# Strassen products in alternating half order, an earlier split, two more tiles and a two-queue start, in a one-layer hybrid trunk

## The chip, the cores and the metric

The kernel runs on one core of one Trainium2 chip. The metric is the device time of one launch in microseconds. Five engines work side by side, each through its own queue in order: TensorE (PE, with its weight loads shown apart as PEld), VectorE (DVE), ScalarE (ACT), GpSimd (POOL) and SyncE (SP). SP only issues DMAs here; ACT and POOL issue some of their own.

## The reference, cut to what matters

One layer over 512 tokens of width 2048, in fp32: a token mixer (one input projection, split between a gated DeltaNet group of 8 heads and a gated short convolution, then an output projection), cross-attention of 4 heads into 256 memory tokens, and a feed-forward part with a width-3 causal convolution.

```python
h = rmsnorm(x, mix_norm);  proj = h @ w_mix_in
y_gdn = gdn_group(proj, gdn_conv, a_log, dt_bias, out_gain)   # conv4 + silu, l2norm, gated delta rule in chunks
y_sc  = b_gate * causal_dwconv(c_gate * hh, sc_conv)
x = x + concat([y_gdn, y_sc]) @ w_mix_out
h = rmsnorm(x, xattn_norm);  mem_n = rmsnorm(mem, mem_norm)
x = x + softmax((h @ w_q) @ (mem_n @ w_k).T * d**-0.5) @ (mem_n @ w_v) @ w_o   # by heads
h = rmsnorm(x, ffn_norm)
u = causal_dwconv(h @ w_up, conv_w);  gate, up = split(u)
x = x + (silu(gate) * up) @ w_down
return rmsnorm(x, final_norm)
```

## The kernel before

Every large matrix product is made in three (or, for products of halves of the tokens, two and a half) passes: a 128x1024 piece of weights `wst` is loaded by DMA, rounded by ACT to a high part `whi` (L523, L146), and DVE subtracts to get the low part `wlo` (L524, L147). The pools hold three `whi`, three `wlo` and five `wst` buffers, so the splitting can run at most three pieces ahead of TensorE. The activations are kept as a 128x512 operand that holds a high part (columns 0 to 255) beside a low part (256 to 511).

`mm2s` (L168) multiplies one piece of eight 128x128 blocks: first eight matmuls of `whi` against all 512 columns (the "wide" ones, L172), then eight of `wlo` against the 256 high columns (the "narrow" ones, L175).

The program goes through these stages, in order of time:

- **Start** (0 to about 101 us): dummy matmuls `warm` on ones, while the first loads arrive; then the values of the memory, `values` (L357). Its first two tiles alternate wide and narrow matmuls (`mm2`, L165 and L166) on parts split by `early_parts`, in the hand-written order of a `manual_schedule`.
- **Fold of values and output weights** (about 101 to 194 us, L681 to L684).
- **Mixer input projection** (about 194 to 740 us): 28 "quads". A quad takes two column tiles of the weights, 2x2 blocks, and makes the four block results by Strassen's seven products (`quad_left`, `quad_right`, each product through `product` and `mm2s`). The products of a quad use, in turn, the blocks a11, a12, s2, s1, s3, a12 changed, a22; s1, s2 and s3 are sums of blocks, made by DVE (L601, L625) and by accumulating DMAs of POOL (L536, L542). The hooks `between[0]` to `between[3]` run the rest of the quad before (convolutions, gating) at four places of a quad.
- **Keys** (about 740 to 842 us, `psk`), and the **fold of keys and queries** (about 842 to 980 us, `pswk`, L1089, L1091, L1097: all narrow). Each of the 32 pieces of `w_xq` takes half of the sixteen key tiles `kts`: q = 0 uses the first eight, q = 1 the last eight. **Mixer output** follows (`psx1`, about 980 to 1187 us). Woven into these three are the chains of the delta rule, `prepare_chunk`, `invert`, `solve`, `recur`, `scaled`, for two halves `hb` of the heads and four chunks `j`. A chain is a generator: `yield cost, wait` gives the time that its step is thought to take on TensorE, and how long it then stays aside. `tick` and `place` run it between the matmuls once the wait is over. So the waits in these yields set where a step stands in the program.
- **Attention** (about 1188 to 1374 us), then **up projection** of the feed-forward part (about 1374 to 2238 us): 44 quads of the same kind, where `run_held` makes the convolutions and the sums of the quad before, and the down projection (to the end, `psd`, all wide).

Outside the hand-written parts a scheduler with a cost table of its own sets the order on each engine, and it may also move single matmuls of one product ahead of another.

Three names return below. `solve` (L924) loads decay rows into `gb`; for chunk j it takes one of two fixed tiles, `xacc` or `macc`, by j % 2. POOL multiplies by `gb` at the end of `solve` (L970, L971), and only then can the load for chunk j + 2 begin. `tp` is the pool of 64 tiles of 128x512 from which `T` takes. `vn` (L991) is the product in `recur` on which the next matmuls, `pso` (L1000), wait.

## Time and profile before

| | |
|---|---|
| median of 3 runs | 2669.97 us (2668.78 to 2670.71) |
| profiled execution | 2670.58 us, span from first to last instruction 2668.4 us |
| mean granted TensorE clock | 0.997 |
| PE busy | 2649.2 us, 99% |
| PEld busy | 2289.6 us, 86% |
| DVE busy | 2238.2 us, 84% |
| ACT busy | 1570.2 us, 59% |
| DMA | 543.91 MB, mean 204 GB/s |

The busy time of a pipelined PE counts overlapping durations, so it says only that PE hardly ever stands still; how fast matmuls follow each other is read from their starts. In a row of the timeline the first number is the start in us, the second the length of the merged group, then engine, line, operation, output and inputs, shape and count; in brackets stands how long the engine had been idle before, and what ended that.

### The profile page before, as it was taken

The page shows a single profiled execution, that of the slowest core. Times are in us where ns is not written, and L with a number is a line of the kernel's source. Part 1 is how long each engine was busy: PE and PEld are TensorE (multiplying, and loading weights), DVE is VectorE, ACT ScalarE, POOL GpSimd, SP SyncE. Part 2 cuts the span into 40 slices and gives each one's busy share as a digit, 9 for nine tenths or more (in the row PEclk, how much of TensorE's full clock was granted, in tenths as well). Part 3 has the DMA queues.
Part 4 walks back from the last instruction along what each step waited for, and adds up shares of the span by engine and source line. Part 5 has one row for each costly group of instructions (what it writes and reads, how often), then busy time and mean ns, then how long its engine had stood idle before and what let it go on. Part 6 is the DMA issues. An engine that isn't in the chain of part 4 may idle for free.

```text
span 2668.4 us, 40148 instructions
## 1 busy us (share of the span) xinstructions
PE 2649.2 (99%) x14757; PEld 2289.6 (86%) x14757; DVE 2238.2 (84%) x3339; ACT 1570.2 (59%) x2284; POOL 238.6 (9%) x281
## 2 busy tenths in 40 slices
PE   9999999999999999999999999999999999999998
PEld 8888888888888998888888888888888888888886
DVE  7878888999988774466779999999999999877888
ACT  7675555666664674445666665565656555554445
POOL 0000000000110222000000000000000000000202
PEclk9999999999999999999999999999999999999999
DMA  8786667777677985665656767777677676764987
GB/s 302 230 272 188 178 159 187 185 195 189 188 228 229 294 252 168 225 201 191 177 164 168 206 178 185 188 178 202 168 197 184 174 200 202 259 192 143 268 272 185
DMA packets 258549, 543.91 MB, mean 204 GB/s; under 512 B 28064, under 2 KB 119344, under 8 KB 258352
## 3 DMA queue, kind: packets, MB, share of 16 engines
q1 hardware_dynamic: 183488, 396.08, 45.3%
q0 software_dynamic: 30176, 93.36, 20.1%
q10 hardware_dynamic: 44688, 51.92, 5.5%
q8 instruction: 115, 1.88, 0.3%
q14 instruction: 82, 0.67, 0.1%
HBM read 472.83 MB, written 67.39 MB: 202 GB/s over the span
## 4 chain that ended last, share of the span: by engine, by line
PE 96%; DVE 2%; DMA 1%; issue 0%; ACT 0%; SPq 0%; DVEq 0%; ACTq 0%
PE px L172 19%; PE px L175 10%; PE pz L172 10%; PE psd L1513 5%; PE psd L1514 5%; PE psd L1517 5%; PE pz L175 5%; PE py L172 5%; PE psx L157 3%; PE psx L158 3%; PE psx L159 3%; PE py L175 2%; PE psk L1069 2%; PE psk L172 2%; PE psk L1072 1%; PE psmo L681 1%
## 5 line engine op out<-in xcount | busy, mean ns | idle before, releaser
L172 PE MATMUL px<-xo,whi 128*128 128x512 f32 x2288 | 574.1, 393 | 1.7 <-ACT whi L523 1.7
L523 ACT CAST whi<-wst 128x1024 fp32r<-128x1024 f32 x290 | 304.2, 1051 | 323.0 <-PE pz L172 186.2
L172 PEld LDWEIGHTS px<-xo,whi 128*128 128x128 f32 x2288 | 411.6, 189 | 76.8 <-ACT whi L523 2.3
L524 DVE TENSOR_TENSOR wlo<-wst,whi 128x1024 fp32r<-128x1024 f32 x290 | 352.7, 1217 | 24.8 <-ACT whi L523 24.8
L175 PEld LDWEIGHTS px<-xo,wlo 128*128 128x128 f32 x2288 | 312.1, 190 | 22.5 <-DVE wlo L524 0.3
L147 DVE TENSOR_TENSOR wlo<-wst,whi 128x1024 fp32r<-128x1024 f32 x204 | 250.0, 1232 | 90.1 <-ACT whi L146 85.6
L175 PE MATMUL px<-xo,wlo 128*128 128x256 f32 x2288 | 319.2, 282 | 0.0
L523 ACT CAST whi<-s 128x1024 fp32r<-128x1024 f32 x214 | 223.3, 1045 | 157.9 <-DVE wlo L524 82.1
L146 ACT CAST whi<-wst 128x1024 fp32r<-128x1024 f32 x204 | 212.6, 1050 | 145.2 <-PE psx L158 35.5
L172 PE MATMUL pz<-xo,whi 128*128 128x512 f32 x1152 | 289.3, 393 | 0.0
L524 DVE TENSOR_TENSOR wlo<-s,whi 128x1024 fp32r<-128x1024 f32 x214 | 260.4, 1218 | 2.6 <-ACT whi L523 2.4
L1514 PE MATMUL psd<-whi,hdl 128*128 128x512 f32 x616 | 239.8, 389 | 0.0
L1513 PE MATMUL psd<-whi,hdh 128*128 128x512 f32 x616 | 239.8, 389 | 0.0
L172 PEld LDWEIGHTS pz<-xo,whi 128*128 128x128 f32 x1152 | 207.1, 189 | 36.9 <-ACT whi L523 0.2
L1517 PE MATMUL psd<-wlo,hdh 128*128 128x512 f32 x616 | 169.3, 390 | 0.3 <-DVE wlo L1308 0.2
L175 PEld LDWEIGHTS pz<-xo,wlo 128*128 128x128 f32 x1152 | 157.1, 190 | 11.4 <-DVE wlo L524 0.2
L1305 ACT CAST whi<-wst 128x1024 fp32r<-128x1024 f32 x96 | 101.2, 1054 | 108.0 <-issue 46.9
L175 PE MATMUL pz<-xo,wlo 128*128 128x256 f32 x1152 | 160.7, 282 | 0.0
L172 PE MATMUL py<-xo,whi 128*128 128x512 f32 x560 | 140.2, 392 | 0.0
L1517 PEld LDWEIGHTS psd<-wlo,hdh 128*128 128x128 f32 x616 | 115.6, 188 | 25.1 <-DVE wlo L1308 1.1
L1514 PEld LDWEIGHTS psd<-whi,hdl 128*128 128x128 f32 x616 | 115.7, 188 | 24.1 <-DVE hdl L153 0.2
L1513 PEld LDWEIGHTS psd<-whi,hdh 128*128 128x128 f32 x616 | 115.6, 188 | 23.9
(374 smaller groups left out, 4948.4 us busy)
## 6 DMA issues: line engine op xcount, KB each, us to landing
wst<-in_w_up SPq DMA_DIRECT2D x132, 512.0 KB, 4.3
wst<-in_w_dn SPq DMA_DIRECT2D x118, 512.0 KB, 4.5
s<-in_w_up POOLq DMA_DIRECT2D x87, 512.0 KB, 6.2
wst<-in_w_mix SPq DMA_DIRECT2D x84, 512.0 KB, 5.4
s<-in_w_mix POOLq DMA_DIRECT2D x55, 512.0 KB, 6.0
s<-in_w_up SPq DMA_DIRECT2D x43, 512.0 KB, 4.6
hid<-hf_d SPq DMA_DIRECT2D x77, 256.0 KB, 5.2
wst<-in_w_xo SPq DMA_DIRECT2D x32, 512.0 KB, 4.6
```

The lines of the kernel that those rows point to most:

```text
L146: nc.scalar.copy(hi, st)
L147: nc.vector.tensor_tensor(lo, st, f(hi), op=ALU.subtract)
L157: nc.tensor.matmul(ps, wh, xh, start=first, stop=False)
L158: nc.tensor.matmul(ps, wh, xl, start=False, stop=False)
L172: nc.tensor.matmul(ps, hi[:, k * P : (k + 1) * P], x, start=first and k == 0, stop=False, skip_group_check=True)
L175: nc.tensor.matmul(ps[:, n:], lo[:, k * P : (k + 1) * P], x[:, :n], start=False, stop=end, skip_group_check=True)
L523: nc.scalar.copy(hi, t)
L524: tt(lo, t, f(hi), op=ALU.subtract)
L1305: nc.scalar.copy(hi[:, i * n : (i + 1) * n], t)
L1513: nc.tensor.matmul(bs[b], xs[0][:, c], w[0][:, n], start=first, stop=False)
L1514: nc.tensor.matmul(bs[b], xs[1][:, c], w[0][:, n], start=False, stop=False)
L1517: nc.tensor.matmul(bs[b], xs[0][:, c], w[1][:, n], start=False, stop=last)
```

## The change

1. `mm2s` takes a flag `swap`, and `product` flips it at every call. One product does its eight wide matmuls and then its eight narrow ones, the next its eight narrow ones and then its eight wide ones, so that like follows like across the border of two products. The flag is reset to False ahead of the 28 and of the 44 quads. The values at the start keep the old order.
2. In a quad after the first two, s2 is split (`wsplit`) ahead of `between[1]`, where the held convolutions stand.
3. `tp` has 66 tiles, and `solve` takes its decay rows for chunks 2 and 3 from it.
4. The first four pieces of `w_xq` go (0, 0), (1, 0), (0, 1), (1, 1), so that two pieces use the first eight key tiles before any uses the last eight.
5. The steps of `prepare_chunk` for the second half of the heads stay aside 14 after their loads instead of 9, and `invert` of that half starts at 130 instead of 145 in the chains' clock.
6. At the start ACT issues the loads of the first columns and of the first two memory tiles, ahead of its table load and its copy; SP begins with the weights. There are 10 dummy matmuls instead of 12.

```diff
-WARM = 12
+WARM = 10
-    tp = ctx.enter_context(tc.tile_pool(name="tp", bufs=64))
+    tp = ctx.enter_context(tc.tile_pool(name="tp", bufs=66))
-    nc.sync.dma_start(cols[:, :C_FFNN], g["cols"][:, :C_FFNN])
+    nc.scalar.dma_start(cols[:, :C_FFNN], g["cols"][:, :C_FFNN])
-    nc.scalar.copy(cst[:, 2:3], cst[:, 0:1])
-    def mm2s(ps, hi, lo, xs, first, last):
+    def mm2s(ps, hi, lo, xs, first, last, swap=False):
         n = xs[0].shape[1] // 2
-        for k, x in enumerate(xs):
-            nc.tensor.matmul(ps, hi[:, k * P : (k + 1) * P], x, start=first and k == 0, stop=False, skip_group_check=True)
-        for k, x in enumerate(xs):
-            end = last and k == len(xs) - 1
-            nc.tensor.matmul(ps[:, n:], lo[:, k * P : (k + 1) * P], x[:, :n], start=False, stop=end, skip_group_check=True)
+        for low in (swap, not swap):
+            dst, w = (ps[:, n:], lo) if low else (ps, hi)
+            for k, x in enumerate(xs):
+                opens, closes = first and low == swap and k == 0, last and low != swap and k == len(xs) - 1
+                nc.tensor.matmul(dst, w[:, k * P : (k + 1) * P], x[:, :n] if low else x, start=opens, stop=closes, skip_group_check=True)
...
     with tc.manual_schedule(engines={mybir.EngineType.Activation, mybir.EngineType.DVE, mybir.EngineType.SP}):
-        load_mem(0)
+        for i in range(2):
+            load_mem(i, nc.scalar)
+        nc.scalar.copy(cst[:, 2:3], cst[:, 0:1])
         for c in (0, S):
             for q in range(2):
                 early_load(0, q, c, c + S)
-            load_mem(c // S + 1)
+        load_mem(2)
...
-        mm2s(ps, *w, xop[r], first, True)
+        mm2s(ps, *w, xop[r], first, True, swaps[0])
+        swaps[0] = not swaps[0]
...
         together(ga)
-        between[1]()
+        if pos < 2:
+            between[1]()
...
-        product(px, wsplit(s2), 6, False)
+        w6 = wsplit(s2)
+        if pos > 1:
+            between[1]()
+        product(px, w6, 6, False)
...
         gb, k, q = load_decay(hb, j), load4("k", 1, hb, j), load4("q", 0, hb, j)
-        yield 0, 9.0
+        yield 0, 9.0 + 5.0 * hb
...
-        gb = cpool.tile([P, S], F32, tag=("xacc", "macc")[j % 2], name=nm("gb"))
+        gb = cpool.tile([P, S], F32, tag=("xacc", "macc")[j], name=nm("gb")) if j < 2 else T("gb")
...
-    order += [g["w_xq"][i, q] for i in range(KT) for q in range(2)]
+    turns = [(0, 0), (1, 0), (0, 1), (1, 1)] + [(i, q) for i in range(2, KT) for q in range(2)]
+    order += [g["w_xq"][i, q] for i, q in turns]
...
-        weave(invert(hb), 20.0 + hb * 125.0)
+        weave(invert(hb), 20.0 + hb * 110.0)
...
-    for i in range(KT):
+    for i, q in turns:
```

How the instructions move. On PE, in the second quad of the up projection (its second and third product; `wlo_14044` and `wlo_14042` are the same low parts of a12, `whi_14074` and `whi_14072` the high, `wlo_14073` the low part of s2), before:

```order
L175 MATMUL py_14047<-xo_13440,wlo_14044 128x256
L175 MATMUL py_14047<-xo_13561,wlo_14044 128x256
L175 MATMUL py_14047<-xo_13682,wlo_14044 128x256
L175 MATMUL py_14047<-xo_13817,wlo_14044 128x256
L172 MATMUL px_14024<-xo_12971,whi_14074 128x512
L172 MATMUL px_14024<-xo_13092,whi_14074 128x512
L172 MATMUL px_14024<-xo_13213,whi_14074 128x512
L172 MATMUL px_14024<-xo_13334,whi_14074 128x512
```

and after (`whi_14102` is the high part of s1, for the fourth product):

```order
L174 MATMUL py_14045<-xo_13438,wlo_14042 128x256
L174 MATMUL py_14045<-xo_13561,wlo_14042 128x256
L174 MATMUL py_14045<-xo_13680,wlo_14042 128x256
L174 MATMUL py_14045<-xo_13815,wlo_14042 128x256
L174 MATMUL pz_14101<-xo_12966,whi_14102 128x512
L174 MATMUL px_14022<-xo_12969,wlo_14073 128x256
L174 MATMUL px_14022<-xo_13090,wlo_14073 128x256
L174 MATMUL px_14022<-xo_13211,wlo_14073 128x256
```

The narrow matmuls of the third product now come first, and here, unlike at most borders, the scheduler put one wide matmul of the fourth product between them.

On DVE, at the border of the second and third quad of the up projection (`s_2611` is s2 of the third quad, L524 and L527 make low parts, L1366 and L1375 the convolutions, `wlo_14226` and `wlo_14224` belong to the third quad's first product), before:

```order
L524 TENSOR_TENSOR wlo_14226<-wst_14216,whi_14225 128x1024
L1366 SCALAR_TENSOR_TENSOR ucv_14130<-uu_14126,cols,ucv_14130 128x511
L572 TENSOR_TENSOR ub_14124<-ub_14124 128x256
L1366 SCALAR_TENSOR_TENSOR ucv_14130<-uu_14126,cols,ucv_14130 128x510
L627 TENSOR_TENSOR gb_14094<-pz_14103,gb_14094 128x512
L1388 TENSOR_TENSOR h_2589_14134<-ucv_14099,ucv_14130 128x512
L572 TENSOR_TENSOR gb_14094<-gb_14094 128x256
L635 TENSOR_TENSOR ua_14202<-px_14024,ua_14202 128x256
L1373 TENSOR_TENSOR ug_14205<-ga_14041,rsy_13937 128x256
L1373 TENSOR_TENSOR ug_14205<-gb_14094,rsy_13937 128x256
L524 TENSOR_TENSOR wlo_14249<-wst_14220,whi_14248 128x1024
L1366 SCALAR_TENSOR_TENSOR ucv_14208<-ug_14205,cols,ucv_14208 128x511
```

and after:

```order
L629 TENSOR_TENSOR ub_14122<-px_14022,ub_14122 128x512
L606 TENSOR_TENSOR s_2611_14269<-s_2599_14211,wst_14214 128x1024
L1375 SCALAR_TENSOR_TENSOR ucv_14128<-uu_14124,cols,ucv_14128 128x511
L576 TENSOR_TENSOR ub_14122<-ub_14122 128x256
L1375 SCALAR_TENSOR_TENSOR ucv_14128<-uu_14124,cols,ucv_14128 128x510
L635 TENSOR_TENSOR gb_14092<-pz_14101,gb_14092 128x512
L1397 TENSOR_TENSOR h_2589_14132<-ucv_14097,ucv_14128 128x512
L576 TENSOR_TENSOR gb_14092<-gb_14092 128x256
L643 TENSOR_TENSOR ua_14200<-px_14022,ua_14200 128x256
L1382 TENSOR_TENSOR ug_14203<-ga_14039,rsy_13935 128x256
L1382 TENSOR_TENSOR ug_14203<-gb_14092,rsy_13935 128x256
L527 TENSOR_TENSOR wlo_14224<-wst_14214,whi_14223 128x1024
```

The subtraction that makes s2 (L606, before L601, which stood behind all rows of the first piece) went ahead of the held convolution, and the low part for the third quad's first product went from its front to its end.

On SP, in the fold of keys and queries (`gb` are decay rows of `solve`, `xd` and `v` its other loads, `ab` and the `xb` the loads of `invert` for the second half of the heads), before:

```order
L143 DMA wst_9734<-in_w_xq 128x1024
L1052 DMA yg_9340<-ysc_d 128x512
L1052 DMA yg_9342<-ysc_d 128x512
L843 DMA k_9389<-qkvz_d 128x4x128
L843 DMA q_9391<-qkvz_d 128x4x128
L143 DMA wst_9804<-in_w_xq 128x1024
L143 DMA wst_9875<-in_w_xq 128x1024
L927 DMA gb_9022<-gc_d 128x512
```

and after:

```order
L912 DMA ab_9026<-nd_d_79 128x1x512
L912 DMA ab_9028<-nd_d_79 128x1x512
L915 DMA xb_9030<-in_idb 128x512
L142 DMA wst_9343<-in_w_xq 128x1024
L142 DMA wst_9381<-in_w_xq 128x1024
L936 DMA gb_9086<-gc_d 128x512
L852 DMA v_9088<-qkvz_d 128x4x128
L939 DMA xd_9090<-xd_d_80 128x4x32
```

The decay rows for chunk 2 (`gb_9022`, now `gb_9086`) stand ahead of that chunk's `v` and `xd`, where before they stood 23 rows behind them, and the loads of `invert` stand just ahead of them.

More of the change, by code (lines that the diff above doesn't have):

```diff
@@ L166, in mm2 @@
         nc.tensor.matmul(ps[:, n:], wl, x[:, :n], start=False, stop=last, skip_group_check=True)
-    def mm2s(ps, hi, lo, xs, first, last):
+    def mm2s(ps, hi, lo, xs, first, last, swap=False):
         n = xs[0].shape[1] // 2
-        for k, x in enumerate(xs):
-            nc.tensor.matmul(ps, hi[:, k * P : (k + 1) * P], x, start=first and k == 0, stop=False, skip_group_check=True)
-        for k, x in enumerate(xs):
-            end = last and k == len(xs) - 1
-            nc.tensor.matmul(ps[:, n:], lo[:, k * P : (k + 1) * P], x[:, :n], start=False, stop=end, skip_group_check=True)
+        for low in (swap, not swap):
[3 more added lines that the diff above has]
+                nc.tensor.matmul(dst, w[:, k * P : (k + 1) * P], x[:, :n] if low else x, start=opens, stop=closes, skip_group_check=True)
+    swaps = [False]
     def proj(src, xs, ps, kt=KT, per=8, ready=None):
@@ L272, in trunk, with load_mem @@
     m2s = [T("mem") for _ in range(KT // 2)]
-    def load_mem(i):
-        nc.sync.dma_start(m2s[i].rearrange("p (k m) -> p k m", k=2), g["mem"][2 * i : 2 * i + 2].rearrange("k p m -> p k m"))
+    def load_mem(i, queue=nc.sync):
+        queue.dma_start(m2s[i].rearrange("p (k m) -> p k m", k=2), g["mem"][2 * i : 2 * i + 2].rearrange("k p m -> p k m"))
     def mem_parts(i):
@@ L805, in some_parts @@
             mem_parts(i)
+    swaps[0] = False
     for pos, (_, _, kind, i) in enumerate(quads):
@@ L1075, in trunk @@
     yp, yl = [], []
-    for i in range(KT):
-        if 8 <= i < 12:
+    for i, q in turns:
+        if q == 0 and 8 <= i < 12:
             yl += [loaded(ysc_d[2 * (i - 8) + n]) for n in range(2)]
-        if 9 <= i < 13:
+        if q == 0 and 9 <= i < 13:
             yp += [split(yl[2 * (i - 9) + n], "yp") for n in range(2)]
-        for q in range(2):
-            hi, lo = piece()
-            ps = PM("pswk")
-            for hh in range(2):
-                for k in range(4):
-                    c = slice(hh * S + k * P, hh * S + (k + 1) * P)
-                    kt = kts[8 * q + 4 * hh + k]
-                    dst = ps[:, hh * NMEM : (hh + 1) * NMEM]
-                    nc.tensor.matmul(dst, hi[:, c], kt[:, :NMEM], start=k == 0 and hh == 0, stop=False, skip_group_check=True)
-                    place(0.12)
-                    nc.tensor.matmul(dst, hi[:, c], kt[:, NMEM:], start=False, stop=False, skip_group_check=True)
-                    place(0.12)
-            for hh in range(2):
-                for k in range(4):
-                    c = slice(hh * S + k * P, hh * S + (k + 1) * P)
-                    dst = ps[:, hh * NMEM : (hh + 1) * NMEM]
-                    nc.tensor.matmul(dst, lo[:, c], kts[8 * q + 4 * hh + k][:, :NMEM], start=False, stop=hh == 1 and k == 3, skip_group_check=True)
-                    place(0.12)
-            wk = T("wk")
-            nc.scalar.activation(wk, ps, AF.Identity, scale=col(C_XN + i))
-            nc.scalar.dma_start(wk_d[i][:, q * S : (q + 1) * S], wk)
@@ new lines, in trunk @@
+        hi, lo = piece()
+        ps = PM("pswk")
+        for hh in range(2):
+            for k in range(4):
+                c = slice(hh * S + k * P, hh * S + (k + 1) * P)
+                kt = kts[8 * q + 4 * hh + k]
+                dst = ps[:, hh * NMEM : (hh + 1) * NMEM]
+                nc.tensor.matmul(dst, hi[:, c], kt[:, :NMEM], start=k == 0 and hh == 0, stop=False, skip_group_check=True)
+                place(0.12)
+                nc.tensor.matmul(dst, hi[:, c], kt[:, NMEM:], start=False, stop=False, skip_group_check=True)
+                place(0.12)
@@ new lines, in trunk @@
+        for hh in range(2):
+            for k in range(4):
+                c = slice(hh * S + k * P, hh * S + (k + 1) * P)
+                dst = ps[:, hh * NMEM : (hh + 1) * NMEM]
+                nc.tensor.matmul(dst, lo[:, c], kts[8 * q + 4 * hh + k][:, :NMEM], start=False, stop=hh == 1 and k == 3, skip_group_check=True)
+                place(0.12)
+        wk = T("wk")
+        nc.scalar.activation(wk, ps, AF.Identity, scale=col(C_XN + i))
+        nc.scalar.dma_start(wk_d[i][:, q * S : (q + 1) * S], wk)
@@ L1441, in norm_rows @@
             r2.append(norm_begin([acc2]))
+    swaps[0] = False
     for i in range(NF):
```

## Prediction, made before the changed kernel was run

> **What bounds the kernel now.** I read the page first: the busy line and the chain that ended last.
>
> ```profile
> PE 2649.2 (99%) x14757; PEld 2289.6 (86%) x14757; DVE 2238.2 (84%) x3339; ACT 1570.2 (59%) x2284; POOL 238.6 (9%) x281
> PE 96%; DVE 2%; DMA 1%; issue 0%; ACT 0%; SPq 0%; DVEq 0%; ACTq 0%
> ```
>
> TensorE is the bound nearly everywhere. So the time can fall in two ways only: matmuls that follow each other faster, and fewer places where PE stands still. For the first I read the timeline of PE, start to start. A steady product of a quad:
>
> ```profile
> 600.00 2.00 PE L172 MATMUL pz<-xo,whi 128*128 128x512 f32 x8
> 601.84 1.11 PE L175 MATMUL pz<-xo,wlo 128*128 128x256 f32 x8
> 602.79 2.00 PE L172 MATMUL px<-xo,whi 128*128 128x512 f32 x8
> ```
>
> Eight wide matmuls take 1.84 us, eight narrow ones 0.95, a product 2.79. Where one width goes on:
>
> ```profile
> 947.25 1.12 PE L1097 MATMUL pswk<-kth,wlo 128*128 128x256 f32 x8
> 948.21 0.28 PE L1089 MATMUL pswk<-kth,whi 128*128 128x256 f32 x1
> ...
> 2300.22 1.07 PE L1517 MATMUL psd<-wlo,hdh 128*128 128x512 f32 x4
> 2302.94 1.07 PE L1517 MATMUL psd<-wlo,hdh 128*128 128x512 f32 x4
> ```
>
> Narrow alone: 8 in 0.96 us, 0.120 each. Wide alone: from the one L1517 group to the next lie 12 matmuls (these 4, and 4 each of L1513 and L1514) in 2.72 us, 0.2267 each. Eight and eight would be 1.813 + 0.96 = 2.77, yet the product takes 2.79. So 0.02 us is lost per product, in its wide half (1.84 against 1.813).
>
> For the second I read the waits of PE, its largest rows:
>
> ```profile
> PE pso L1000 <- DVE vn L991: 2.0, 1, 2.0
> PE px L172 <- ACT whi L523: 1.7, 2, 1.0
> PE psk L165 <- ACT ewh L152: 1.1, 1, 1.1
> ```
>
> Each stands for a place that an edit touches. There is little else to win.
>
> **The runs of sixteen.** Is the 0.02 us paid per change of width, or per narrow matmul? In the second case longer runs save nothing. One place tells them apart, where the order has a wide run of three between two narrow ones:
>
> ```profile
> 1424.50 1.11 PE L175 MATMUL px<-xo,wlo 128*128 128x256 f32 x8
> 1425.45 0.86 PE L172 MATMUL pz<-xo,whi 128*128 128x512 f32 x3
> 1426.15 1.11 PE L175 MATMUL pz<-xo,wlo 128*128 128x256 f32 x8
> 1427.10 2.00 PE L172 MATMUL px<-xo,whi 128*128 128x512 f32 x8
> ```
>
> Three wide take 0.70 us (0.68 when steady): already 0.02 of the loss. If a debt of the narrow matmuls were worked off, the rest of it would have come on top after the next eight; but the product at 1427.10 takes 1.84 us for its wide half, as always. So the loss sits at the front of a wide run and does not pile up. In the built orders a wide run follows a narrow one 594 times before and 352 times after: 242 fewer, at 0.02 us, is 4.8 us. Bounds: nothing, and (rounding of the rows, 0.025) 6.0. I take 4.8.
>
> [...]
>
> **What the swap asks of DVE.** A product that begins narrow needs its `wlo` 1.84 us earlier. The tight case of the mixer quads, and the tightest usual place of a late quad:
>
> ```profile
> 615.22 1.21 DVE L524 TENSOR_TENSOR wlo<-s,whi 128x1024 fp32r<-128x1024 f32 x1
> 616.76 2.00 PE L172 MATMUL px<-xo,whi 128*128 128x512 f32 x8
> ...
> 1718.78 1.22 DVE L524 TENSOR_TENSOR wlo<-s,whi 128x1024 fp32r<-128x1024 f32 x1
> 1721.77 0.40 PE L172 MATMUL px<-xo,whi 128*128 128x512 f32 x1
> ```
>
> The low parts are ready at 616.43 and 1720.00, 0.33 and 1.77 us ahead of the product's start. So a narrow-first product there finds them in time. Its `whi` buffer comes free 0.95 us later than now, but the product three places on, which reuses it, is then wide-first, with its `wlo` due only 1.84 us after its start. What hides this edit is thus a lead of 0.3 to 1.8 us; without it each lost 0.1 us would cost 25 us over some 250 narrow-first products. I take 0 in the steady quads.
>
> The first up quads are another matter, since DVE has the norm and four convolutions to make up there.
>
> ```profile
> 1400.75 2.07 PE L172 MATMUL px<-xo,whi 128*128 128x512 f32 x8
> 1400.87 1.22 DVE L524 TENSOR_TENSOR wlo<-s,whi 128x1024 fp32r<-128x1024 f32 x1
> ...
> 1421.41 2.12 PE L172 MATMUL px<-xo,whi 128*128 128x512 f32 x8 [0.69 <-ACT whi L523]
> 1442.23 2.11 PE L172 MATMUL px<-xo,whi 128*128 128x512 f32 x8 [1.01 <-ACT whi L523]
> ```
>
> Now PE waits 0.69 and 1.01 us (0.2 more each, from start to start) at the s2 of the third and fourth quad, both of which the early split takes away: in the order of the changed program s2 is made before the convolution. But the s2 of the second quad, which is not moved, becomes narrow-first: its `wlo` ends at 1402.09, 1.34 us after the product's start, less one wide matmul (0.23) that the order puts ahead. And in the third quad the same DVE rows now stand ahead of the first `wlo`: adding the starting distances of these rows (0.33, 0.6, 0.66, 1.14 us by length) from 1410 on, it comes about 1 us after it is due, and the next product about 0.3. So -2.1 +1.1 +1.0 +0.3 = +0.3 us. Bounds: -2.1 and +3.
>
> **The fold and the chains.** Three stalls, each with its cause:
>
> ```profile
> 849.01 0.28 PE L1091 MATMUL pswk<-kth,whi 128*128 128x256 f32 x1
> 850.28 0.39 PE L1089 MATMUL pswk<-kth,whi 128*128 128x256 f32 x1 [0.99 <-ACT kth L350]
> 850.91 0.39 PE L1091 MATMUL pswk<-kth,whi 128*128 128x256 f32 x1 [0.24 <-DVE kth L351]
> 865.25 0.66 PE L836 MATMUL pskt<-mk,k 128*128 128x128 f32 x4 [0.72 <-DMA k<-qkvz_d]
> ...
> 919.34 0.28 PE L1089 MATMUL pswk<-kth,whi 128*128 128x256 f32 x1
> 921.65 2.08 PE L1000 MATMUL pso<-dt,vn 128*128 128x128 f32 x8 [2.04 <-DVE vn L991]
> 925.09 0.56 PE L1091 MATMUL pswk<-kth,whi 128*128 128x256 f32 x1
> 927.37 0.32 PE L1091 MATMUL pswk<-kth,whi 128*128 128x256 f32 x1
> ```
>
> At 849 the last key tile is late: (1.27 - 0.12) + (0.63 - 0.12) = 1.7 us. With two pieces of the first eight key tiles in front (some 5.8 us of PE), it is there in time: -1.7. At 864 a chain of the second half asks for keys whose load has not landed: 0.7 us, which the 5 units of longer waiting cover.
>
> At 919 the idle 2.2 us is the smaller part:
>
> ```profile
> 920.60:927.40 6.80, 5.75 (x27) 5.75 (x28) 4.90 (x9) 2.60 (x6) 3.91 (x3) 0.50 0.77 213
> ...
> 909.16 1.39 POOL L970 TENSOR_TENSOR qd<-gb,q 128x512 f32<-128x512 f32 x1
> 913.29 0.38 SPq L927 DMA_DIRECT2D gb<-gc_d  x1
> 918.35 0.63 ACT L968 ACTIVATE gb<-gb 128x512 f32<-128x512 f32 x1 [2.59 <-DMA gb<-gc_d]
> ...
> 914.45 1.06 PE L832 MATMUL pv<-v,pt 128*128 128x128 f32 x8
> ```
>
> The first row is the window after it: granted clock 0.50. The 16 small matmuls from 921.65 take 3.44 us to 925.09, where eight at the full clock (914.45) take 1.06 with the end of the last, some 1.8 for sixteen started, so 1.6 lost; then 11 narrow in 2.28 us instead of 1.32. With 2.2 idle that is 4.8 us. The cause is a decay load that could be issued only after POOL was done with the tile of two chunks before (ACT then waits 2.59 us for it, and DVE's `vn` behind ACT). In the changed order that load takes a tile of its own and stands 23 rows further ahead. So -4.8, if nothing takes its place.
>
> What is late next: `invert` of the second half starts 15 units earlier, so its 62 DVE operations fall among the first half's `solve` and `recur`, whose `vn` PE awaits; and its loads on SP stand just ahead of two weight loads and of `gb` and `v` behind them, waiting for POOL's stores. Nothing in the trace prices this; bounds are 0 and another stall like that at 919, 4.8. Nearest is the pair of small ones, 0.7 and 1.7, so I take 2.5 given back. Sum of this part: -1.7 -0.7 -4.8 +2.5 = -4.7.
>
> **The start.** PE stands still mostly for two loads:
>
> ```profile
> 7.21 0.62 ACT L152 CAST ewh<-wst 128x512 fp32r<-128x512 f32 x1 [1.62 <-DMA wst<-in_w_xv]
> 9.93 0.91 ACT L282 ACTIVATE mw<-mem,cols 128x256 fp32r<-128x256 f32 x2 [1.09 <-DMA mem<-in_mem]
> GB/s 0 0 0 0 0 49 33 35 148 365 400 413 340 290 217 224 321 277 246 290 359 293 344 353 347 369 391 362 416 378 334 344 356 388 422 435 403 416 362 356
> ```
>
> The last row is the first 13 us in 40 slices. From 2.9 us on the transfers run at 217 to 435 GB/s; only the 1.3 us before are slow (33 to 49), while the narrow `cols` head the one queue. With two queues the weights fill that gap, but the same bytes must land before the third memory tile (9.93), which is what holds the rest. So -1.0; bounds 0 and -2.7 (both waits). The two dummy matmuls less only shorten what PE does ahead of the first load.
>
> **The sum**, against the profiled execution's 2670.6 us: -4.8 +0.3 -4.7 -1.0 = -10.2, so 2660.4; that execution lies 0.6 above the median of 2669.97, so 2659.8, said as 2660.
>
> **Rivals.** (a) *The loss goes with each narrow matmul, or sixteen in a row cost more than two eights*: the rest of the sum stays, 2664.6. Against it stand the rows at 1424. [...] (b) *The chains' stalls come back elsewhere, with the half clock*: PE's order has many places where a small matmul waits for DVE, and 2.2 us of idle were enough for the half clock: 2.3 more than what I gave back, or with two of them up to +7: 2662 to 2667. (c) The other side: *narrow-first products wait for DVE all along*. The place is the up projection, where DVE is 84% busy or more, the mechanism that the due time of `wlo` moves by 1.84 us while the lead is 0.3 to 1.8. It decides from 0.04 us per narrow-first product (0.04 x 250 = 10 us, the whole gain); at 0.1 us the time is 2685. For it speaks the lead of 0.33 at 616; against it the 1.77 that is usual. (d) *The change does not do what it says*: excluded for the runs by the order; for the start, 2661.
>
> **How the numbers follow.** Forecast 0.65, (a) 0.08, (b) 0.16, (c) 0.11; (d) lies inside the forecast. No change is 0.2% or 5.3 us either side of 2670, so faster means below 2664.6. Faster: 0.62 of the forecast, 0.04 of (a), 0.09 of (b), together 0.75; same: what is left of these and 0.03 of (c), 0.17; slower: the rest of (c), 0.08. The range: below, 2654, when nothing is given back in the chains (-2.5), the start gives its bound (-1.7) and the up quads 1.5 more; above, 2668, which takes in (a), (b) and the mild part of (c).
>
> **What would show it.** Right: wide halves in runs of sixteen, two products in 5.57 us instead of 5.59; no PE wait on L350's successor or on the `vn` of the first half, and no window of clock 0.50 in the fold; the first weights' cast before 7 us. Wrong: PE rows that wait for DVE's `wlo` (L527) in quad after quad, or a window of clock 0.50 elsewhere between 840 and 1110 us.

## The result, and the profile after

| | before | after |
|---|---|---|
| median of 22 runs, us | 2670.56 (2665.82 to 2673.34) | 2665.26 (2662.23 to 2668.84) |
| ratio to before, 95% interval | | 0.9982, 0.9975 to 0.9988 |
| profiled execution, us | 2670.58 | 2664.10 |
| its span, us | 2668.4 | 2662.0 |

The change gains 4.8 us by the ratio (3.2 to 6.7), or 0.18%; 10 were predicted, so the time lies inside the predicted range of 2654 to 2668, 5 us above the forecast of 2660. The two profiled executions differ by 6.5.

Both programs issue the same 14,745 matmuls behind the dummies, and outside the fold each stage starts at the same count. So the trace can be cut at the same matmuls in both (lengths in us, from the start of one stage to the start of the next; the last column is what each stage gained or lost):

| stage | before | after | difference |
|---|---|---|---|
| the first 250 matmuls (the start) | 53.59 | 53.39 | -0.20 |
| values, up to the first mixer quad | 140.29 | 140.43 | +0.14 |
| mixer quads | 546.02 | 544.65 | -1.37 |
| keys, fold, chains, mixer output, first 34 us of attention | 482.01 | 479.60 | -2.41 |
| the rest of attention, norm, first 52 up products (seven quads and three products) | 301.54 | 301.76 | +0.22 |
| the other 256 up products | 715.09 | 712.53 | -2.56 |
| down projection | 419.69 | 419.40 | -0.29 |

This table, with one column for each experiment, is the measure used below: where an edit does not touch them, the mixer and up stages repeat within 0.1 us (the start and the down projection vary by up to 2), while medians of whole runs carry an uncertainty of about 2. The keys-to-attention stage repeats less well: in the changed kernel and three variants of it whose edits leave the fold alone it takes 479.5 to 481.0.

So what is sure of the gain is 1.4 in the mixer and 2.6 in the up quads, 3.9 of the 4.8. All else together comes to 0.9 by the medians, with an interval from -0.7 to 2.8: the runs do not tell that apart from nothing.

From the page after, the busy line and the chain that ended last: PE is the bound as before.

```profile
PE 2641.6 (99%) x14755; PEld 2289.1 (86%) x14755; DVE 2256.8 (85%) x3339; ACT 1570.0 (59%) x2284; POOL 241.6 (9%) x281
PE 94%; DVE 2%; DMA 2%; ACT 1%; issue 1%; SPq 0%; POOL 0%; DVEq 0%; ACTq 0%; POOLq 0%
```

The timeline of PE after, in steady mixer quads: sixteen narrow in two groups, then sixteen wide. From 598.12 to 603.69 two products take 5.57 us, start to start; before it was 2 x 2.79.

```profile
598.12 1.11 PE L174 MATMUL px<-xo,wlo 128*128 128x256 f32 x8
599.08 1.12 PE L174 MATMUL pz<-xo,wlo 128*128 128x256 f32 x8
600.03 2.00 PE L174 MATMUL pz<-xo,whi 128*128 128x512 f32 x8
601.88 1.98 PE L174 MATMUL px<-xo,whi 128*128 128x512 f32 x8
603.69 0.52 PE L174 MATMUL px<-xo,wlo 128*128 128x256 f32 x3
```

The waits of PE after (total us, times, longest). The `vn` of 2.0, the two `whi` of 1.7 and the `kth` of before are gone; a `pt` of 2.7 is new and the largest, and there are `ga`, `vn`, `wlo` and `whi` of 0.6 to 1.0.

```profile
PE pv L841 <- DVE pt L975: 2.7, 1, 2.7
PE psk L164 <- DVE mw L284: 1.5, 1, 1.5
PE px L174 <- ACT ga L588: 1.0, 2, 0.7
PE pso L1009 <- DVE vn L1000: 0.9, 1, 0.9
PE px L174 <- DVE wlo L527: 0.9, 1, 0.9
PE pz L174 <- ACT whi L526: 0.6, 1, 0.6
```

Windows of the trace after, in the start and around the new `pt` wait in the fold. In a row stand the window, its length, the busy us of PE, PEld, DVE, ACT and POOL with their counts, and then PEclk, the granted clock. Both times a stretch in which PE was busy for less than half is followed by one at clock 0.50.

```profile
5.00:8.30 3.30, 1.55 (x6) 0.61 (x4) 2.12 (x5) 2.68 (x6) 0.00 (x0) 1.00 1.07 386
8.40:11.80 3.40, 3.40 (x12) 2.91 (x12) 3.26 (x8) 2.95 (x7) 0.00 (x0) 0.50 1.05 378
916.40:919.70 3.30, 1.09 (x9) 1.09 (x10) 3.21 (x8) 0.67 (x2) 0.35 (x1) 1.00 1.02 333
919.80:923.10 3.30, 3.30 (x17) 3.30 (x17) 3.21 (x6) 1.69 (x3) 1.37 (x2) 0.50 1.10 366
```

### The profile page after: what moved, and what is told of

It reads as the page before. It is cut to its first block, busy times and chain, and to the rows that moved or that the text cites. A ratio compares the mean times of both kernels' runs of the same rounds, so it can differ in the third digit from the quotient of the medians.

```text
span 2662.0 us, 40226 instructions
## 1 busy us (share of the span) xinstructions
PE 2641.6 (99%) x14755; PEld 2289.1 (86%) x14755; DVE 2256.8 (85%) x3339; ACT 1570.0 (59%) x2284; POOL 241.6 (9%) x281
## 4 chain that ended last, share of the span: by engine, by line
PE 94%; DVE 2%; DMA 2%; ACT 1%; issue 1%; SPq 0%; POOL 0%; DVEq 0%; ACTq 0%; POOLq 0%
PE px L174 30%; PE pz L174 15%; PE py L174 7%; PE psd L1523 5%; PE psd L1527 5%; PE psd L1524 5%; PE psk L174 3%; PE psx L156 3%; PE psx L157 3%; PE psx L158 3%; PE psk L1079 2%; PE psk L1082 1%; PE pss L1175 1%; PE pss L1177 1%; PE pss L1176 1%; PE psmo L689 1%
## 5 line engine op out<-in xcount | busy, mean ns | idle before, releaser
L174 PE MATMUL px<-xo,whi 128*128 128x512 f32 x2288 | 564.5, 391 | 1.0 <-ACT ga L588 1.0
L174 PEld LDWEIGHTS px<-xo,whi 128*128 128x128 f32 x2288 | 420.1, 188 | 83.6 <-ACT ga L588 2.4
L527 DVE TENSOR_TENSOR wlo<-wst,whi 128x1024 fp32r<-128x1024 f32 x290 | 354.1, 1223 | 41.8 <-ACT whi L526 40.9
L146 DVE TENSOR_TENSOR wlo<-wst,whi 128x1024 fp32r<-128x1024 f32 x204 | 255.7, 1260 | 89.1 <-ACT whi L145 88.1
L174 PEld LDWEIGHTS px<-xo,wlo 128*128 128x128 f32 x2288 | 301.1, 191 | 13.1 <-DVE wlo L527 1.6
L527 DVE TENSOR_TENSOR wlo<-s,whi 128x1024 fp32r<-128x1024 f32 x214 | 261.3, 1222 | 4.7 <-ACT whi L526 4.5
```

The costliest lines, as they stand in the source:

```text
L146: nc.vector.tensor_tensor(lo, st, f(hi), op=ALU.subtract)
L174: nc.tensor.matmul(dst, w[:, k * P : (k + 1) * P], x[:, :n] if low else x, start=opens, stop=closes, skip_group_check=True)
L527: tt(lo, t, f(hi), op=ALU.subtract)
```

## The experiments

Stage lengths from the traces, in us (one execution each), and medians of 11 runs (12 for the tiles, 5 for the inversion at 125; 22 for the first two rows). The ratios go against runs of the kernel before beside each experiment, whose medians were 2669.78 to 2670.06. "C" is keys to attention, "D" attention to the first up quads, "E" the other up quads, cut as in the table above. A stage length is that of the profiled execution alone. Those of e5, e6, e8 and e12 were the slowest of their runs, 2.6 to 3.9 us above the median, and that of the changed kernel was 1.2 below its own; so a stage difference there is not a difference of medians.

| kernel | start | mixer | C | D | E | median | ratio to before, 95% |
|---|---|---|---|---|---|---|---|
| before | 53.59 | 546.02 | 482.01 | 301.54 | 715.09 | 2670.56 | 1 |
| after | 53.39 | 544.65 | 479.60 | 301.76 | 712.53 | 2665.26 | 0.9975 to 0.9988 |
| e1 runs alone | 54.07 | 544.63 | 481.92 | 301.85 | 712.53 | 2667.78 | 0.9983 to 1.0001 |
| e2 fours | 54.11 | 547.65 | 482.23 | 301.23 | 718.51 | 2673.66 | 1.0008 to 1.0025 |
| e3 after, inversion at 125 | 52.70 | 544.63 | 508.10 | 301.74 | 712.53 | 2691.19 | 1.0065 to 1.0090 |
| e4 after, first up quads wide-first | 52.19 | 544.63 | 480.40 | 302.35 | 712.53 | 2665.18 | 0.9974 to 0.9992 |
| e5 before with the tiles | 53.44 | 546.02 | 491.32 | 301.64 | 715.09 | 2675.35 | 1.0012 to 1.0029 |
| e6 after, both times as before | 52.23 | 544.65 | 488.83 | 301.76 | 712.53 | 2669.21 | 0.9988 to 1.0005 |
| e7 after, key rows by halves | 54.41 | 544.65 | 479.52 | 301.75 | 712.53 | 2664.80 | 0.9973 to 0.9990 |
| e8 after, s2 behind | 53.51 | 544.63 | 480.95 | 304.29 | 712.53 | 2666.07 | 0.9974 to 0.9991 |
| e9 before with the times | 52.64 | 546.02 | 485.04 | 301.52 | 715.09 | 2672.72 | 0.9998 to 1.0016 |
| e10 after without the tiles | 53.02 | 544.66 | 483.18 | 301.84 | 712.53 | 2666.92 | 0.9979 to 0.9997 |
| e11 after, thinner inversion | 53.34 | 544.63 | 480.83 | 303.33 | 712.53 | 2666.74 | 0.9979 to 0.9997 |
| e12 after, late rows, 12 dummies | 52.37 | 544.63 | 482.00 | 301.80 | 712.53 | 2663.44 | 0.9969 to 0.9988 |

**Is it the change of width?** First the runs alone, in the kernel before:

```
+    def mm2s(ps, hi, lo, xs, first, last, swap=False):   # as in the change
...
+        mm2s(ps, *w, xop[r], first, True, swaps[0])
+        swaps[0] = not swaps[0]
```

> The kernel before with the runs of sixteen alone (243 changes from narrow to wide fewer). Theory (each such change costs 0.020 us, whatever stands around it): two products take 5.567 us instead of 5.587, together -4.9 us; given back 0.2 at the first mixer quad, 0.9 at the entry to the keys, and 1 to 2.5 in the first up quads, where the two waits for s2 stay and narrow-first products add theirs: about 2668.5, 2 us under the kernel before. Rival (the loss belongs to the narrow matmuls and not to the change): 5.587 stays and the time is 2 to 4 us above the kernel before.

Two products take 5.567 us, start to start, against 5.587. E falls from 715.09 to 712.53: 128 pairs of products, 0.020 us each. So the saving needs none of the other edits. Not all of it shows in the time, which is not told apart from that of the kernel before: C is no shorter, although the wait for keys at 864 is absent here, and D is 0.3 longer although it holds 26 pairs of products.

Then the other way, in the kernel before:

```
+        for h in range(0, len(xs), 4):
+            for k in range(h, h + 4):
+                nc.tensor.matmul(ps, hi[...], xs[k], ...)
+            for k in range(h, h + 4):
+                nc.tensor.matmul(ps[:, n:], lo[...], xs[k][:, :n], ...)
```

> The kernel before with each product issued as four wide, four narrow, four wide, four narrow: 524 changes from narrow to wide more. Theory (0.020 us per change): a product takes 2.813 us instead of 2.793, together +10.5 us, 2681. Rival (the loss goes with the number of narrow matmuls worked off in a wide run, so half as many narrow ones cost half): 2.793 stays, 2670.5 give or take 1.

The timeline of PE, four wide and four narrow in turn: from 1800.71 to 1803.52 one product takes 2.81 us.

```profile
1800.71 1.09 PE L173 MATMUL pz<-xo,whi 128*128 128x512 f32 x4
1801.64 0.63 PE L176 MATMUL pz<-xo,wlo 128*128 128x256 f32 x4
1802.11 1.09 PE L173 MATMUL pz<-xo,whi 128*128 128x512 f32 x4
1803.04 0.64 PE L176 MATMUL pz<-xo,wlo 128*128 128x256 f32 x4
1803.52 0.86 PE L173 MATMUL px<-xo,whi 128*128 128x512 f32 x3
```

E gives the mean: 715.09 to 718.51 over 256 products, 0.0134 us for the second change in a product; in the mixer 0.008. So neither expectation holds: the time of a product is 2.783 at half a change, 2.793 at one and 2.807 at two. Against 2.773 for a product without any change (the prediction's rows of one width), a change costs 0.020 us behind eight or sixteen narrow matmuls, and 0.014 to 0.017 behind four. The step of the prediction (0.020 each) was right for the runs that the change makes, not as a law for any run. Why a change of width costs time, and why less in the mixer, no run here shows.

**The first up quads.** Narrow-first products wait for `wlo` there, so I took them back for three quads of the changed kernel:

```
-        swaps[0] = not swaps[0]
+        swaps[0] = not (swaps[0] or hold[0])
...
+        hold[0] = i in (0, 1, 2)
```

> The changed kernel with all products of the first three up quads begun wide; the runs of sixteen begin with the fourth. Theory (the waits at 1396 to 1416 us are for low parts that a narrow-first product needs 1.8 us earlier): these four waits, 2.8 us together, go; 8 changes of width more cost 0.2; 2.6 us less, 2662.7. Rival (DVE is late there whatever the order, because of the norm and the held convolutions): the waits move to the high or low parts a product later, less than 1 us gained.

The rival holds: PE's waits are other ones, of the same size, up to the fourth quad, and D is 0.6 longer.

```profile
1417.17 2.14 PE L174 MATMUL px<-xo,whi 128*128 128x512 f32 x8 [0.68 <-ACT whi L526]
1439.02 1.22 PE L174 MATMUL px<-xo,wlo 128*128 128x256 f32 x8 [0.17 <-DVE wlo L527]
1440.91 0.96 PE L174 MATMUL px<-xo,whi 128*128 128x512 f32 x3 [0.68 <-ACT gb L614]
1447.56 1.21 PE L174 MATMUL pz<-xo,wlo 128*128 128x256 f32 x8 [0.80 <-DVE wlo L527]
```

The third busy number of a window says why. From 1400 to 1425 us DVE (the third) has no free time in the kernel before, and in this one as well; so a wait there may only tell which of its rows PE happens to need. The kernel before:

```profile
1400.00:1425.00 25.00, 24.31 (x138) 20.99 (x137) 25.00 (x38) 17.40 (x23) 1.71 (x2) 1.00 0.58 154
```

The changed kernel with wide-first quads (the changed kernel itself has 24.52):

```profile
1400.00:1425.00 25.00, 24.32 (x138) 20.93 (x137) 25.00 (x37) 16.87 (x24) 2.13 (x3) 1.00 0.56 138
```

And s2 put back behind the held convolutions:

```
-        if pos < 2:
-            between[1]()
+        between[1]()
```

> The changed kernel with s2 split behind the held convolutions again. Theory A (DVE is full from 1400 to 1425 us, 25.0 us of 25, and TensorE waits for it somewhere in any order): the waits move to s2 of the third and fourth quad, the sum stays within 0.4 us, 2665.3. Theory B (the prediction's step: each of these two waits is worth 1.0 us of its own, less the 1.3 of late low parts that the order ahead brings): 0.8 us more, 2666.1.

D is 304.29. Of the 2.5 us more, some 1.6 are not the edit's: a half clock from 1418.5 to 1421.9 us, which e11, with the up quads of the changed kernel, has at the same place (D 303.33). What stays is 1.0, and the trace has one new wait for it, at 1465 us (0.68, for `gb`), not the two at s2. That is nearer to B in size and to A in kind. Since it rests on one execution each, it is an indication.

**The fold.** The prediction named the decay rows' tile as the cause of the stall at 919. The tiles alone, in the kernel before:

```
-    tp = ... bufs=64
+    tp = ... bufs=66
...
-        gb = cpool.tile([P, S], F32, tag=("xacc", "macc")[j % 2], name=nm("gb"))
+        gb = cpool.tile([P, S], F32, tag=("xacc", "macc")[j], name=nm("gb")) if j < 2 else T("gb")
```

> The kernel before with the two more tiles for decay rows alone. Theory (the wait of 2.2 us at 919 us and the half clock behind it came from the decay load that waited for POOL to be done with the tile of two chunks before): both go, 4.8 us less, 2665. Rival (DVE's vn is late there for DVE's own queue, and the decay load is only what shows): the wait and the half clock stay, 2670.

This is the clearest miss: the median is 5.4 us higher, and C of the profiled execution grows by 9.3. That execution has 17.1 us at half clock in C against 6.8 before; by an estimate, half of the 10.2 more, 5.1 us, is what they cost. From its waits of PE, and from the timelines of POOL and ACT:

```profile
PE pso L1000 <- DVE vn L991: 6.3, 2, 3.9
```

```profile
916.29 1.27 POOL L971 TENSOR_TENSOR k<-gb,k 128x512 f32<-128x512 f32 x1 [3.49 <-DMA k<-qkvz_d]
917.52 2.79 POOL L970 TENSOR_TENSOR qd<-gb,q 128x512 f32<-128x512 f32 x2
```

```profile
918.98 0.63 ACT L1018 ACTIVATE q<-q 128x512 f32<-128x512 f32 x1 [5.87 <-POOL qd L970]
919.51 1.03 ACT L146 CAST whi<-wst 128x1024 fp32r<-128x1024 f32 x1
```

The decay load of chunk 2 does go out early, at 882.61 us instead of 913.29, as meant, and ACT's wait for it now lies where PE waits for nothing:

```profile
882.61 0.43 SPq L927 DMA_DIRECT2D gb<-gc_d  x1
889.60 0.63 ACT L968 ACTIVATE gb<-gb 128x512 f32<-128x512 f32 x1 [2.56 <-DMA gb<-gc_d]
```

But at the old place ACT now stands 5.87 us for POOL's `qd`; its next cast (the second row, at 919.51 us) and DVE's `wlo` and `vn` are late behind it, and PE waits 3.9 us instead of 2.0. Two things ended just as `qd` started, at 917.52. By the releaser that the profile names, its tile of the shared ring had held a `wk`, and the store of that (`wk_d<-wk`, 5.4 us) ended at 917.50; and POOL was busy until 917.56 with a `k` that stood ahead of `qd` and had waited 3.49 us for its load. Either alone would have held `qd` as long, so which of them counts is open. The decay load, at any rate, was the last to arrive before, and not the only one that was late.

Next the start times alone, then the changed kernel without the tiles:

```
-        yield 0, 9.0
+        yield 0, 9.0 + 5.0 * hb
...
-        weave(invert(hb), 20.0 + hb * 125.0)
+        weave(invert(hb), 20.0 + hb * 110.0)
```

> The kernel before with the second half's two start times alone (inversion at 110, 14 units of waiting in its chunks), tiles and everything else as before. Theory A (the stall at 919 us went with the times: the second half's inversion is then under way before the first half's solves, and TensorE's and DVE's rows meet differently): the wait of 2 us at 919 and most of the half clock go, 3 to 4 us less than before, 2666. Theory B (times and tiles only work together: without tiles of their own the decay rows stand still with POOL, now behind an inversion that has begun): the stall stays or grows, 2670 to 2675.

> The changed kernel without the two more tiles for decay rows. Theory A (the tiles move the ring so that POOL waits for stores of wk, as with the tiles alone, where they cost 5 us): without them the fold is 1 to 3 us shorter, 2663. Theory B (beside the earlier inversion the tiles are what keeps the decay load ahead of POOL): ACT waits for the decay rows of the third and fourth chunk again, a wait of 2 us or more and the half clock, 2668.

And the changed kernel with both times as before, and with only the inversion's time as before:

> The changed kernel with both start times of the second half as before (9 units of waiting in its chunks, inversion at 125), so that of the fold's edits only the tiles and the keys' order stay. Theory (the stall at 915 us came with the earlier inversion, the late end of the run with the inversion at 125 came from the longer waiting in front of it): no wait over 1.5 us and no half clock between 840 and 1110; the 0.7 us wait for keys at 864 is back; 3.7 us less than the changed kernel, 2661.5. Rival (DVE has the same steps to do in the fold wherever they start): a wait of over 2 us with the half clock stays somewhere in the fold, 2664 to 2666.

> The changed kernel with the second half's inversion started at 125 again instead of 110. Theory (the stall at 915.7 us is DVE working off the inversion's steps ahead of the solve that TensorE waits for; the decay rows' own tiles have removed the stall of before): that wait of 2.7 us goes, the half clock of 3.4 us behind it, worth 1.7, and the 0.6 and 0.9 us waits after it: 4 to 5 us less, 2661. Rival (DVE has the same work in the fold wherever the inversion starts): a stall of like size comes elsewhere between 900 and 1000 us, 2665 give or take 1.

In e9 the `vn` wait at 919 went, but two others came, at 917 (`pt`) and 943 (`vn`), each with about 2 us:

```profile
PE pv L832 <- DVE pt L966: 2.2, 1, 2.2
PE pso L1000 <- DVE vn L991: 2.1, 1, 2.1
```

Its median of 2672.7 lies where B has it, but the interval of its ratio includes 1, and ACT's waits for decay loads are only 0.4 and 0.6 us there: the gain of A is refuted, B is not shown. e10 is B in kind: ACT waits 2.13 us for a decay load at 922.6 us again, PE has the two waits of e9, and a half clock follows the second. Its time, 2666.9, lies between A and B. e6 is the rival in kind and worse (one wait of 4.4 us for `vn` and 10.2 us at half clock, 2669); e3 is neither. C in all combinations, of one execution each:

| C, us | tiles as before | two more tiles |
|---|---|---|
| times as before | 482.01 (before) | 491.32 (e5) |
| times as before, keys by halves | not run | 488.83 (e6) |
| new times | 485.04 (e9) | not run |
| new times, keys by halves | 483.18 (e10) | 479.60 (after) |

So the `vn` stall at 919 went with the new start times, with the tiles and without them, and stayed where only the tiles were changed or the times put back (e5, e6). (e3, which has of the new times only the longer waiting, keeps 0.9 us of it.) Wherever it went, a `pt` wait of 1.2 to 2.8 us stands within 6 us of its place. By the medians the tiles cost 5.4 us with the old times, and with the new ones they are not told apart from nothing (e10 against after: 2666.9 and 2665.3); the new times with the tiles gain 4 (e6 against after). Without the tiles the changed kernel waits 2.2 us for `vn` at 940 us (at most 1.5 in its variants with them):

```profile
PE pso L1009 <- DVE vn L1000: 2.2, 1, 2.2
PE pv L841 <- DVE pt L975: 2.0, 1, 2.0
```

And the two new times belong together. With the longer waiting but the inversion at 125 (e3) the stall at 915 is small (1.38 us from start to start instead of 2.94, with no half clock), as expected; but PE then waits for mixer output rows again and again between 1097 and 1215 us; C is 28.5 us longer than in the changed kernel. Its largest wait:

```profile
PE psx L156 <- DVE x0r L1129: 11.7, 9, 2.9
DVE x0r L1129 <- DMA x0r<-xp_d: 48.9, 14, 5.1
```

DVE in turn waits there for rows that are loaded back (`xp_d`), 48.9 us in all against 2.6 in the changed kernel. Late chains are not the reason by themselves: the last `pso` comes at 1072 us here, and at 1080 in e5 and 1074 in e6, which have no such row of waits. Why these loads are late is open.

The keys by halves were predicted to be worth 1.7. In the two pairs of the table C is 2.5 (491.32 to 488.83) and 1.9 us (485.04 to 483.18) shorter with them, but most of that lies elsewhere: in the first 72 us of the fold, where the wait stood, it is 1.1 and 1.4. The wait on `kth` is in the traces of the kernel before and of the four with its order (e1, e2, e5, e9) and in none with the new.

**The new stall.** In the changed kernel's timeline of DVE, the `pt` that PE waits for stands behind two splits of y rows, a weight's `wlo` and the steps of the second half's inversion (`tm` and `xb`, not shown here), and DVE goes from one to the next:

```profile
914.70 0.69 DVE L152 TENSOR_TENSOR ypl<-yg,yph 128x512 fp32r<-128x512 f32 x1
916.09 1.22 DVE L146 TENSOR_TENSOR wlo<-wst,whi 128x1024 fp32r<-128x1024 f32 x1
917.22 0.68 DVE L152 TENSOR_TENSOR ypl<-yg,yph 128x512 fp32r<-128x512 f32 x1
918.15 0.40 DVE L975 TENSOR_TENSOR pt<-pt,ps 64x256 f32<-64x256 f32 x1
```

Two tries, thinner steps first, and then the y rows two turns later, together with the two dummy matmuls put back:

```
-                yield 0, 2.75, 0
+                yield 0, 2.75 + 0.55 * hb, 0
...
-        weave(invert(hb), 20.0 + hb * 110.0)
+        weave(invert(hb), 20.0 + hb * 102.0)
```

> The changed kernel with the second half's inversion begun at 102 instead of 110 and its steps 3.3 units apart instead of 2.75, so that it ends when it did. Theory (the stall at 915 us is DVE full with the inversion's steps beside the first half's solves, so thinner steps let the solve's rows through): the 2.7 us wait and its half clock, together 4.4 us, go or shrink to under 1.5: 2661 to 2663. Rival (what TensorE waits for is late because of the loads of queries and yg that DVE's order puts ahead, not because of the number of steps): the wait stays over 2 us, 2665.

```
-WARM = 10
+WARM = 12
...
-        if q == 0 and 8 <= i < 12:
+        if q == 0 and 10 <= i < 14:
...
-        if q == 0 and 9 <= i < 13:
+        if q == 0 and 11 <= i < 15:
```

> The changed kernel with the first eight y rows loaded and split two row pairs later in the fold (4 x 1.4 us of DVE out of the place of the stall), and with twelve dummy matmuls again. Two stages, read apart. Fold: theory (DVE's row of the solve, pt of 64 x 256, stands behind two splits of y rows and a weight's low part): the wait at 915 us falls from 2.9 us to 1.5 or less and its half clock goes, so keys to attention take 476 to 478 us instead of 479.6; rival (the moved splits meet the waits at 930 and 942, or other tiles come round in the ring): 479 to 482. Start: theory (with ten dummies TensorE idles in its first full-clock window and so gets a half-clock window; with twelve it does not): no half clock after the first full one, the first 250 matmuls end by 52.7 us; rival (the grid of windows decides): half clock as before, 53.0 to 53.5. Together 2661 if both hold.

e11 changes nothing at that place: 2.5 us. In e12 the wait is 1.7; but it is 1.6 in e7 too, which leaves the y rows as they are, so this is not shown to be the splits' doing. The half clock stays, the `vn` at 939 grows to 1.5 and mixer output rows wait at 1098 to 1102 with a half clock of their own: C is 482.0. Its start, read apart, came out as the theory says, with no half clock and 52.37 us, but the rival is not excluded by one execution (see the start, below). Its median is the lowest of all, 2663.44, but its interval (0.9969 to 0.9988) overlaps that of the changed kernel: not told apart from it.

**The entry to the keys.** After the mixer the changed kernel loses 0.9 us that no step of the prediction had. In the kernel before, the built order happened to mix the second half of the first key row with the first half of the second row; in the changed one it does not, and PE keeps step with DVE, which makes the weight tiles at 0.40 us each (8 wide in 2.69 us from this start to the next, where 1.84 is usual):

```profile
744.02 2.85 PE L1079 MATMUL psk<-mw,whi 128*128 128x512 f32 x8
746.71 1.11 PE L1082 MATMUL psk<-mw,wlo 128*128 128x256 f32 x8
```

```
-    order += [g["w_xk"][n, i] for n in range(KT) for i in range(2)]
+    keys = [(0, 0), (1, 0), (0, 1), (1, 1)] + [(n, i) for n in range(2, KT) for i in range(2)]
+    order += [g["w_xk"][n, i] for n, i in keys]
```

> The changed kernel with the first two key rows by halves, first half of both, then second half of both, as the built order of the kernel before happened to mix them. Theory (the seven matmuls at 744.5 to 746.7 us that follow each other at 0.40 us instead of 0.23 keep step with DVE, which makes the second eight weight tiles at 0.40 us each): they run at 0.23, 0.9 us less, 2664.4. Rival (the tiles come late by more than the other row's first half covers): the same loss one group later, no change.

The eight run at full speed now, but PE waits 0.64 us for the next `whi`, which ACT makes behind its part of the same tiles; C is 479.52. The rival holds: the loss moved, and the first 88 matmuls of the keys take 16.8 us in both kernels.

```profile
745.09 2.00 PE L1082 MATMUL psk<-mw,whi 128*128 128x512 f32 x8
746.93 1.11 PE L1085 MATMUL psk<-mw,wlo 128*128 128x256 f32 x8
748.68 2.11 PE L1082 MATMUL psk<-mw,whi 128*128 128x512 f32 x8 [0.64 <-ACT whi L145]
```

## Why the prediction was right and wrong

**The runs of sixteen: right, -4.9 for -4.8.** 0.020 us per pair of products, in every trace that has them: 2.56 in E, 1.37 in the mixer, where the next point takes 0.47 off, and by the same price 0.5 in D, where other waits hide it. The rival that the loss goes with each narrow matmul is refuted: the matmuls are the same and only their order changed.

**Steady quads, DVE's lateness: right, 0.** E is 128 x 0.020 to the hundredth, so no narrow-first product waited there. One place was missed, the first mixer quad (0.47 us): there the order had put two wide matmuls of another product ahead of the one whose PSUM tile ACT still reads (`ga`), and the swap took these away.

**The first up quads: +0.7 for +0.3.** D is 0.22 longer and should be 0.52 shorter by its 26 pairs. The waits named came (`wlo` 0.91, `ga` 0.68, `whi` 0.57) and those at s2 went. So the term was small because gains and losses nearly cancelled, not because each was priced: with DVE full there (24.5 to 25.0 of 25 us), taking the order back in e4 only renamed the waits.

**The fold and the chains: -2.4 for -4.7, the step that failed.** "-4.8, if nothing takes its place" rested on the last releaser of one wait, the decay load. Two things were wrong with it. The load was not waiting for its tile when it went out: the prediction's own rows have POOL done at 910.55 us, and the load was issued at 913.29, behind two weight loads in SP's order:

```profile
908.56 4.63 SPq L143 DMA_DIRECT2D wst<-in_w_xq  x2
913.29 0.38 SPq L927 DMA_DIRECT2D gb<-gc_d  x1
```

And making the load early did not take the stall away: e5 has it 31 us earlier and a longer `vn` wait, 3.9 us. The stall went with the new start times (e9), and something did take its place: a wait of 2.7 us that ends at 918.6, a half clock from 919.7 to 923.2, two waits of 0.6 and 0.9 behind, and 0.9 at the entry to the keys. This half clock is a sign that the prediction itself had named for being wrong. By stage C (-1.7 and -0.7 for the key waits, -4.8 for 919) that is 4.8 given back, not 2.5. The mechanism of giving back was named (the inversion's steps among rows that PE awaits; rival (b), 2662 to 2667, is where the time fell), the size taken was that of the small stalls and not that of the large one. Since C differs by 1.4 us between executions with the same fold, and one half-clock window less is an estimated 1.7 of the 2.4, even the sign of what the fold's edits gained beyond that is weakly shown.

**The start: -0.2 in this pair, -0.5 on average, for -1.0.** The first weights' cast came at 6.43 us instead of 7.21, as said. The step that failed is "the two dummy matmuls less only shorten what PE does ahead of the first load": in the changed kernel they leave PE idle for 1.75 us of its first 3.4 us at full clock, and 3.4 us at half clock follow (8.4 to 11.8). So it is in four of the eight traces with ten dummies (after, e8, e10, e11, with 1.5 to 1.75 us idle), those whose full clock began at 4.5 to 5.4 us; in the other four it began at 6.1 us or later, and none follows. In e12, with twelve (from 5.74 us, 1.05 idle), and in the five traces of the old start there is none. That speaks for the dummies, but no run has them changed alone, nor the two queues. The first 250 matmuls take 52.64 to 54.11 us with the old start (mean 53.57) and 52.19 to 54.41 with the new one and ten dummies (53.10), so single pairs tell little.

**The sum.** -10.2 was predicted and -6.5 came in the profiled pair. The 3.7 are 2.3 in C, 0.9 ahead of the mixer (0.8 of it the start), 0.35 in the mixer and 0.45 in D, less 0.3 in the down projection that nothing in the change explains.

## What to carry to other kernels

A term that counts a repeated event, measured on its steady rows, can be trusted to the hundredth of a microsecond; a term that takes away one stall, read from its last releaser, cannot, as long as another engine on the same path is full or waits in order behind other tiles. Ask of each such stall what arrives second, and test each part alone before crediting it: here the tiles that were to take the stall away cost 5.4 us alone. Compare a stage between several executions first, too, before a difference of 2 us in it is believed. Where an engine has no idle time over a stretch (DVE, 25.0 of 25 us), do not price an order there by its single waits; whether less work on that engine would help was not tried here.

## What the runs showed of the hardware

**Steps of the inversion that began during a product of POOL took up to 1.47 us.** In the trace before 7 of the 124 steps and in the trace after 8 of 124 began while POOL ran a product. They ended 0.15 to 0.28 us behind that product and took 0.41 to 1.47 us; the others took 0.18 to 0.43. From e12, DVE and POOL:

```profile
911.53 0.42 DVE L924 TENSOR_TENSOR xb<-xb,tm 128x247 f32<-128x247 f32 x1
911.99 1.40 DVE L923 TENSOR_TENSOR tm<-ab,xb 128x252 f32<-128x252 f32 x1
913.42 1.37 DVE L924 TENSOR_TENSOR xb<-xb,tm 128x252 f32<-128x252 f32 x1
```

```profile
911.62 1.49 POOL L980 TENSOR_TENSOR k<-gb,k 128x512 f32<-128x512 f32 x1 [7.72 <-DMA q<-qkvz_d]
913.06 1.45 POOL L979 TENSOR_TENSOR qd<-gb,q 128x512 f32<-128x512 f32 x1
```

These two steps take 1.40 and 1.37 us, the one ahead of them 0.42: some 1 us more of DVE for each. In the changed kernel a `pt<-pt,ps` at 919.69 us, with one input in PSUM, takes its usual 0.28 us while POOL's `k` runs from 919.35 to 920.80. There two inversion steps at 905 and 906 us, beside POOL's `k` and `qd`, take 1.31 and 1.34, and DVE has no gap from there to the `pt` row at 918. That this is part of the stall is argued, not tested; the prediction had not counted it. Why the one kind of row is longer beside a product and the other is not, no run here shows.

**Half clock came in stretches of 3.41 us or twice that, mostly behind 3.41 us in which PE was idle for 1.4 us or more.** The lengths hold in all traces, but for the last stretch, which runs past the end of the work. In the traces before and after, the granted clock changes only whole multiples of 3.413 us after its first record: that is at 5.84 us before, with changes at 920.61, 927.44 and 2661.41, and at 4.97 us after, with changes at 8.38, 11.80, 919.74, 923.16 and 2657.13. Sorting such stretches of fourteen traces, without the last 20 us or so of each, by how long PE was idle in them by its records: 17 of 18 with 1.7 us or more (half of 3.41) were followed by half clock, 10 of 14 with 1.4 to 1.7, 4 of 29 with 1.0 to 1.4, and 2 of more than ten thousand with less. So the same waits were followed by a half clock in some executions and not in others: at 1416 us the changed kernel has none (of the two stretches there, from 1411.27 and from 1414.68 us, PE is idle for 0.74 and 0.84), and e8 and e11, with the same waits, have one. A half clock of 3.41 us costs some 1.7 us by an estimate (half of it); D of e11 is 1.57 longer than that of the changed kernel.
